# Larger pieces for the adding transfers of a decoder trunk, and a later start of their second group

## The chip, the cores and the metric

The kernel runs on one core of a Trainium2 chip. The metric is the time of one execution on the device in microseconds (us). Besides, one execution was recorded by the hardware profiler; all views quoted below come from that recording.

The engines go by these names: PE multiplies matrices (PEld is its loading of weights), DVE and ACT work elementwise, POOL is the general engine, which here does small column arithmetic and issues some DMA transfers, and SP issues the other transfers. Each engine takes its instructions strictly in the order of its own list; between engines there are only semaphores. "SPq", "ACTq" and "POOLq" mark issues of transfers. All transfers run on the same 16 DMA engines.

## The reference: what is computed

A trunk of two layers over 512 positions of width 1024, everything in float32:

```python
for i in range(DEPTH):                      # DEPTH = 2
    mixer, pre, post = (even_mixer, ...) if i % 2 == 0 else (odd_mixer, ...)
    x = x + rms_norm(mixer(rms_norm(x, pre)), post)
    h = conv_ffn(rms_norm(x, ffn_pre_g[i]), ffn_w_up[i], ffn_conv_w[i], ffn_conv_b[i], ffn_w_down[i])
    x = x + rms_norm(h, ffn_post_g[i])
```

The first mixer joins latent attention (8 heads) and differential attention (4 heads, where two softmaxes are subtracted and each head's output is normalised). The second joins dilated attention (three groups of 4 heads) and stick-breaking attention (4 heads). Each feed-forward block multiplies by `ffn_w_up` (1024 x 5632), applies a causal convolution of width 3, a gate, and `ffn_w_down` (2816 x 1024).

## The kernel before

**Products.** The 512 positions are four row tiles of 128, worked in the order 3, 2, 1, 0. Each float32 operand is split into a rounded high part and a remainder, and a product is three matmuls: high by high, high by low, low by high (`mm3`, L315 to L317). Weights come in units of up to 128 x 1024 floats. SP loads a unit into one of three raw buffers `wraw` (L59, or L57 for a unit of two halves), ACT rounds it into `wh` (L81), DVE subtracts to get `wl` (L82). Five pairs of `wh` and `wl` rotate, so that units are made ahead of use.

**The sums of weight blocks.** For some column tiles of `ffn_w_up` (14 pairs of tiles in layer 0, 12 in layer 1) the block product is done with seven products in place of eight. For that it needs four sums of blocks of these weights. They don't depend on x, and no engine computes them: DMA transfers that add into their destination build them, from one DRAM array (`in_ffn_up_q`) into others (`ws`), long before the feed-forward block reads them through L57. `sum_steps` (L145) lists the transfers. Pairs go in chunks of three, and for each chunk there are eight steps, four that copy and four that add:

```python
steps = [(0, 3, ALU.bypass), (2, 2, ALU.bypass), (0, 2, ALU.add), (2, 0, ALU.add), (1, None, ALU.bypass),
         (1, 0, ALU.add), (3, -1, ALU.bypass), (3, 1, ALU.add)]
```

The list runs step by step, and within a step over the chunks; a step waits for the earlier step on the same chunk. A transfer of a full chunk has 384 rows of 512 floats, which is 768 KB; the last chunk of layer 0 has two pairs, 512 KB. All of them are issued by POOL (L161), because adding transfers are issued there. `max_dma_last_dim` at the issue bounds the length of a piece in bytes. The descriptors that POOL writes for its transfers lie in a space of 1024 bytes, which the kernel sets when it is built (`dynamic_dma_scratch_size=1024`, L1918).

**Where they are issued.** Layer 0 (the first group): `make_sums(0, range(3))` puts the 24 transfers of three chunks into POOL's list in one run, after the normalisation of the latent columns in the first mixer (L1074). The other 16, of two chunks, are put one by one among the work units of differential attention. Layer 1 (the second group): `make_sums(1, range(CHUNKS[1]))`, 32 transfers of four chunks, in one call at L1493, between the first value tiles of the second mixer and its projections. A call begins with a "mark" (L168): a transfer of one float from some tile to the first `ws` chunk. It carries no data that matters; it holds the copies after it back until that tile is written. Before, the second group's mark reads a word of `xl`, the low part of the normalised and transposed x, in the columns of row tile 3, the first of the four to be written.

**What else POOL does.** `rstd` (L226) computes (mean square + eps)^-0.5 of a row tile on POOL: L230, L232 with a second half, L233. Differential attention does the same for each head and row tile (L1262, L1263); the result scales the output on DVE (L1270). At the change from the first feed-forward block to the second mixer, each row tile needs two: one for the block's output (then DVE adds it to x, L815) and one for the next input (then DVE scales it, L819, PE transposes it, L263, ACT and DVE split it into `xh` and `xl`, L223 and L224). These transposes stand among the matmuls of the first value tiles of the second mixer (`av`, one for each row tile; ACT takes each to `vst`, L1484, and sends it on by four transfers, L1486).

The order of POOL's list is written out by hand there (`manual_schedule`) or follows from the program's order and a planner's priorities. In the second group, the mark and the first seven transfers stood among the `rstd` instructions of row tiles 2, 1 and 0.

Of the kernel before, what the change touches and what calls it, by code (L numbers as in the profile page):

```python
# [9 lines left out]
F32 = mybir.dt.float32  # L10
# [7 lines left out]
P = 128  # L18
# [21 lines left out]
CHUNKS = [-(-n // CHUNK) for n in PAIRS]  # L40
# [55 lines left out]
def trunk(tc, A, out):  # L96
    nc = tc.nc
    PE, ACT, DVE, POOL = nc.tensor, nc.scalar, nc.vector, nc.gpsimd

    with ExitStack() as top:  # L100
# [28 lines left out]
        lead = cst.tile([P, 80], F32, tag="lead", name="lead")  # L129
# [15 lines left out]
        def sum_steps(layer, chunks, mark=None):  # L145

            wide = "(a q) c -> a (q c)"
            if layer not in sums_of:
                sums_of[layer] = [[dpool.tile([CHUNK * P, S], F32, tag=f"ws{layer}{j}{c}", name="ws")
                                   for c in range(CHUNKS[layer])] for j in range(4)]  # L150
            tiles = sums_of[layer]

            def move(c, j, src, op):
                n = min(CHUNK, PAIRS[layer] - c * CHUNK) * P
                if src is None:
                    src = tiles[0][c][:n]
                elif src < 0:
                    src = tiles[1][c][:n]
                else:
                    src = A[f"ffn_up_q{layer}"][src, c * CHUNK * P:c * CHUNK * P + n]  # L160
                nc.gpsimd.dma_start(tiles[j][c][:n].rearrange(wide, q=4), src.rearrange(wide, q=4), accum_op=op,  # L161
                                    max_dma_last_dim=2048)

            steps = [(0, 3, ALU.bypass), (2, 2, ALU.bypass), (0, 2, ALU.add), (2, 0, ALU.add), (1, None, ALU.bypass),
                     (1, 0, ALU.add), (3, -1, ALU.bypass), (3, 1, ALU.add)]
            moves = [lambda c=c, step=step: move(c, *step) for step in steps for c in chunks]
            if mark is not None:
                moves.insert(0, lambda: nc.gpsimd.dma_start(tiles[0][chunks[0]][0:1, 0:1], mark))  # L168
            return moves

        def make_sums(layer, chunks, mark):
            with tc.manual_schedule(engines={POOL.engine}):
                for move in sum_steps(layer, chunks, mark):
                    move()
# [1233 lines left out]
        def odd(xnT, pending, order):  # L1408
            xh, xl = xnT
            with ExitStack() as es:  # L1410
# [59 lines left out]
                for i in ORDER:  # L1470
# [12 lines left out]
                    st = chp.tile([P, 512], F32, tag="s", name="vst")  # L1483
# [6 lines left out]
                nc.scalar.dma_start(tab12[:], A["dil_tab12"])  # L1490
                DVE.tensor_copy(tri[:], trif[:])

                make_sums(1, range(CHUNKS[1]), xl[0:1, 0, 3 * P:3 * P + 1].bitcast(F32))  # L1493


                for u in range(2):
# [321 lines left out]
        xnT = even()  # L1818
        xnT = ffn(0, *xnT, False)
        xnT = odd(*xnT)  # L1820
        ffn(1, *xnT, True)

# [103 lines left out]
```

## Time and profile before

| | |
|---|---|
| median of 3 runs | 1184.62 us (1179.21 to 1190.16) |
| the profiled execution | 1182.12 us, span 1180.3 us |
| mean granted PE clock | 0.983 of full |
| PE busy | 1122.2 us, 95% of the span |
| DVE, ACT, POOL busy | 888.1, 629.8, 118.2 us |
| moved by DMA | 201.48 MB, mean 171 GB/s |
| issued by POOL | 72 transfers of sums and 2 marks |

The span is what the profile covers; the time of the same execution is 1.8 us longer. POOL's rows show when it issued a transfer and for how long. "issue" as the end of a wait means that the engine waited for nothing that the profile shows. Columns are explained where rows are quoted.

### The profile page before, as it was taken

What the parts mean: (1) busy time and instruction counts of PE and PEld (TensorE: products, weight loads), DVE (VectorE), ACT (ScalarE), POOL (GpSimd) and SP (SyncE); (2) the same over time, 40 slices, a digit from 0 to 9 for tenths busy, and PEclk for the clock granted to TensorE, in tenths of its full rate; (3) what the DMA queues carried; (4) which work ended last, traced back from release to release, by engine and by line L of the source; (5) the groups of instructions that cost most, each with busy time, mean ns of one, the idle gap of its engine ahead of it and who ended that gap; (6) DMA issues with size and microseconds to landing.
All of it is one profiled execution on the core that took longest, in us unless ns stands there. A gap on an engine that the chain in (4) does not pass through costs nothing.

```text
span 1180.3 us, 17608 instructions
## 1 busy us (share of the span) xinstructions
PE 1122.2 (95%) x6576; PEld 959.9 (81%) x6576; DVE 888.1 (75%) x1504; ACT 629.8 (53%) x1069; POOL 118.2 (10%) x213
## 2 busy tenths in 40 slices
PE   9999909889999999999997999999999999999997
PEld 8876706668899999888886887787989999888886
DVE  6686506528989999988984357566898999879887
ACT  5565506425656666455653355465466666535562
POOL 2211013232000000000023011111100000000001
PEclk9999959989999999999999999999999999999999
DMA  7777867764345656334658987787234655424462
GB/s 285 249 163 160 223 149 221 150 146 147 90 145 178 192 177 190 106 132 143 195 182 275 262 186 209 176 215 170 95 123 146 191 183 178 144 76 143 147 210 76
DMA packets 79541, 201.48 MB, mean 171 GB/s; under 512 B 9056, under 2 KB 10208, under 8 KB 79328
## 3 DMA queue, kind: packets, MB, share of 16 engines
q1 hardware_dynamic: 56352, 142.09, 36.9%
q0 software_dynamic: 21184, 54.53, 21.2%
q10 hardware_dynamic: 1920, 3.74, 1.0%
q8 instruction: 52, 0.85, 0.3%
q14 instruction: 33, 0.27, 0.1%
HBM read 192.95 MB, written 60.85 MB: 215 GB/s over the span
## 4 chain that ended last, share of the span: by engine, by line
PE 74%; issue 16%; POOL 4%; DMA 3%; DVE 1%; ACT 1%; SPq 0%; POOLq 0%; DVEq 0%; ACTq 0%
PE u L315 12%; PE u L317 12%; PE u L316 12%; PE acc L315 6%; PE acc L316 6%; PE acc L317 6%; PE apt L315 2%; PE apt L316 2%; PE apt L317 2%; POOL ws L161 2%; PE ao L317 1%; PE ao L315 1%; PE ao L316 1%; DMA ws<-ws 1%; PE p L317 1%
## 5 line engine op out<-in xcount | busy, mean ns | idle before, releaser
L81 ACT CAST wh<-wraw 128x1024 fp32r<-128x1024 f32 x237 | 245.1, 1047 | 155.7 <-PE u L316 50.0
L82 DVE TENSOR_TENSOR wl<-wraw,wh 128x1024 fp32r<-128x1024 f32 x237 | 287.0, 1219 | 51.4 <-ACT wh L81 50.8
L315 PE MATMUL u<-xh,wh 128*128 128x256 f32 (+1 forms) x664 | 212.0, 319 | 0.0
L316 PE MATMUL u<-xl,wh 128*128 128x256 f32 (+1 forms) x664 | 211.8, 319 | 0.0
L317 PE MATMUL u<-xh,wl 128*128 128x256 f32 (+1 forms) x664 | 211.7, 319 | 0.0
L317 PEld LDWEIGHTS u<-xh,wl 128*128 128x128 f32 x664 | 126.5, 190 | 9.0 <-DVE wl L82 0.3
L315 PEld LDWEIGHTS u<-xh,wh 128*128 128x128 f32 x664 | 126.5, 190 | 8.9 <-ACT wh L81 0.3
L316 PEld LDWEIGHTS u<-xl,wh 128*128 128x128 f32 x664 | 126.5, 190 | 8.7
L317 PE MATMUL acc<-wh,gl 128*128 128x512 f32 (+1 forms) x250 | 96.8, 387 | 0.0
L316 PE MATMUL acc<-wl,gh 128*128 128x512 f32 (+1 forms) x250 | 96.8, 387 | 0.0
L315 PE MATMUL acc<-wh,gh 128*128 128x512 f32 (+1 forms) x250 | 96.8, 388 | 0.0
L317 PE MATMUL u<-gh,wl 128*128 128x256 f32 x312 | 88.3, 283 | 0.0
L315 PE MATMUL u<-gh,wh 128*128 128x256 f32 x312 | 88.3, 283 | 0.0
L316 PE MATMUL u<-gl,wh 128*128 128x256 f32 x312 | 88.3, 283 | 0.0
L230 POOL TENSOR_TENSOR rv<-ms,epst 128x1 f32<-128x1 f32 x39 | 12.7, 326 | 697.4 <-ACT junk L755 320.4
L492 ACT ACTIVATE y<-u,cw 128x512 f32<-128x512 f32 x88 | 67.5, 775 | 14.6 <-PE u L317 14.6
L161 POOL DMA_DIRECT2D ws<-in_ffn_up_q x54 | 46.5, 861 | 282.0 <-issue 271.8
L496 DVE SCALAR_TENSOR_TENSOR y<-u,cw,y 128x511 f32<-128x511 f32 x88 | 65.0, 742 | 6.3 <-ACT y L492 6.3
L498 DVE SCALAR_TENSOR_TENSOR y<-u,cw,y 128x510 f32<-128x510 f32 x88 | 65.5, 746 | 2.3
L315 PEld LDWEIGHTS u<-gh,wh 128*128 128x128 f32 x312 | 59.9, 192 | 0.2
L316 PEld LDWEIGHTS u<-gl,wh 128*128 128x128 f32 x312 | 59.9, 192 | 0.1
L317 PEld LDWEIGHTS u<-gh,wl 128*128 128x128 f32 x312 | 59.9, 192 | 0.0
(362 smaller groups left out, 2456.9 us busy)
## 6 DMA issues: line engine op xcount, KB each, us to landing
ws<-in_ffn_up_q POOLq DMA_DIRECT2D x48, 768.0 KB, 7.3
wraw<-ws SPq DMA_DIRECT2D x104, 256.0 KB, 2.9
wraw<-in_ffn_w_down SPq DMA_DIRECT2D x44, 512.0 KB, 3.5
wraw<-in_ffn_up_q SPq DMA_DIRECT2D x78, 256.0 KB, 2.8
wraw<-in_ffn_w_up SPq DMA_DIRECT2D x36, 512.0 KB, 4.2
ws<-ws POOLq DMA_DIRECT2D x16, 768.0 KB, 6.0
wraw<-in_od_w_dqk SPq DMA_DIRECT2D x12, 512.0 KB, 5.9
wraw<-in_ffn_w_down SPq DMA_DIRECT2D x22, 256.0 KB, 2.9
```

The lines of the kernel that those rows point to most:

```text
L81: self.nc.scalar.copy(h[:, :w], raw[:, :w])
L82: self.nc.vector.tensor_tensor(l[:, :w], raw[:, :w], h[:, :w].bitcast(F32), ALU.subtract)
L161: nc.gpsimd.dma_start(tiles[j][c][:n].rearrange(wide, q=4), src.rearrange(wide, q=4), accum_op=op, max_dma_last_dim=2048)
L230: POOL.tensor_tensor(v[:, :n], ms, epst[:, :n], ALU.add)
L315: PE.matmul(o, lh, rh, start=first, stop=False, skip_group_check=more)
L316: PE.matmul(o, lh, rl, start=False, stop=False, skip_group_check=more)
L317: PE.matmul(o, ll, rh, start=False, stop=last, skip_group_check=more)
L492: ACT.activation(y[:, z], u[z], AF.Identity, bias=c[:, 3:4], scale=c[:, 2:3])
L496: DVE.scalar_tensor_tensor(y[:, z, 1:], u[z][:, :S - 1], c[:, 1:2], y[:, z, 1:], ALU.mult, ALU.add)
L498: DVE.scalar_tensor_tensor(y[:, z, 2:], u[z][:, :S - 2], c[:, 0:1], y[:, z, 2:], ALU.mult, ALU.add)
```

## The change

```diff
@@ sum_steps.move
                 nc.gpsimd.dma_start(tiles[j][c][:n].rearrange(wide, q=4), src.rearrange(wide, q=4), accum_op=op,
-                                    max_dma_last_dim=2048)
+                                    max_dma_last_dim=8192)
...
@@ odd, ahead of the second mixer's projections
                 DVE.tensor_copy(tri[:], trif[:])
 
-                make_sums(1, range(CHUNKS[1]), xl[0:1, 0, 3 * P:3 * P + 1].bitcast(F32))
+                ACT.copy(lead[0:1, 1:2], st[0:1, 0:1])
+                make_sums(1, range(CHUNKS[1]), lead[0:1, 1:2])
```

The first edit changes the bound on a piece from 2 KB to 8 KB for all transfers of `sum_steps`; four rows of 512 floats, which lie one behind another, then make one piece, and a full chunk is 96 rows of 2048 floats. The number of transfers, their bytes and their order among themselves stay.

The second edit changes what the second group waits for. `st` is the tile of the last `av` (row tile 0). ACT copies one float of it into a free column of the constant tile `lead`, after it has sent that tile on, and the mark reads that. In POOL's list the mark and all 32 transfers then stand behind the last `rstd` of the change of layers, in one run; before, the mark and seven transfers stood among those. ACT gains one instruction. The lists of PE, DVE and SP hold the same instructions in the same order.

## The prediction

> **What bounds the kernel now.** I read the page first: the busy times and the two rows of slices (each slice is 29.5 us).
>
> ```profile
> span 1180.3 us, 17608 instructions
> PE 1122.2 (95%) x6576; PEld 959.9 (81%) x6576; DVE 888.1 (75%) x1504; ACT 629.8 (53%) x1069; POOL 118.2 (10%) x213
> PE   9999909889999999999997999999999999999997
> PEclk9999959989999999999999999999999999999999
> ```
>
> PE is the bound nearly everywhere. It is idle for 1180.3 - 1122.2 = 58 us, and the slices say where: the sixth (147 to 177 us) has digit 0, the three after it 9, 8, 8, and the slice at 620 to 649 us has 7. The clock row dips at the same places. The view by windows puts numbers on them; after the window come its length, the busy time of PE, PEld, DVE, ACT, POOL, the granted clock, the DMA engines' busy share, and GB/s.
>
> ```profile
> 147.00:176.00 29.00, 1.66 (x8) 1.04 (x6) 0.73 (x4) 0.00 (x0) 5.58 (x9) 0.60 0.65 153
> 176.00:262.00 86.00, 73.35 (x351) 54.07 (x352) 40.64 (x117) 39.42 (x121) 26.98 (x49) 0.94 0.75 175
> 620.00:650.00 30.00, 23.22 (x105) 18.14 (x104) 14.01 (x19) 9.02 (x17) 9.04 (x17) 0.94 0.84 276
> ```
>
> PE's idle time is 27.3, 12.7 and 6.8 us, together 46.8 of the 58. Both places lie in the two groups of weight sums. Who keeps PE waiting is in the view of waits (engine, what it was about to do, what ended the wait: total us, times, longest).
>
> ```profile
> DVE otok L1270 <- POOL rr L1263: 56.7, 8, 30.4
> PE tpp L906 <- DVE s L1245: 33.3, 4, 27.8
> PE tpp L906 <- DVE odl L224: 5.2, 2, 3.5
> PE tpo L1277 <- DVE otok L1270: 2.1, 1, 2.1
> DVE t L819 <- POOL rr L233: 10.6, 3, 6.0
> PE av L317 <- DVE xl L224: 3.4, 1, 3.4
> ```
>
> At both places DVE waits for an `rr` of POOL, and PE for DVE. The timeline of the first place:
>
> ```profile
> 140.97 0.19 ACT L1260 ACTIVATION_READ_ACCUMULATOR jk<-otok 128x1 f32 x1
> 148.26 0.40 PE L317 MATMUL aqk<-xh,wl 128*128 128x512 f32 x1
> 158.26 0.98 POOL L161 DMA_DIRECT2D ws<-in_ffn_up_q  x1 [4.89 <-issue]
> 166.04 0.97 POOL L161 DMA_DIRECT2D ws<-in_ffn_up_q  x1 [6.80 <-issue]
> 173.20 0.95 POOL L161 DMA_DIRECT2D ws<-in_ffn_up_q  x1 [6.18 <-issue]
> 174.34 0.18 POOL L1262 TENSOR_TENSOR st<-st,epsp 128x1 f32<-128x1 f32 x1
> 175.20 0.35 DVE L1270 SCALAR_TENSOR_TENSOR otok<-otok,rr,subg 128x128 f32<-128x128 f32 x1 [30.36 <-POOL rr L1263]
> ```
>
> ACT has the sum of squares ready at 141.16. POOL takes it up at 174.34, because 24 issues of sums stand ahead of it. DVE, which takes its list in order, stops at the result, and PE runs dry at 148.7. **So the kernel's main loss is POOL's queue of issues, not DMA speed as such.**
>
> **Part 1, larger pieces: why POOL's issues are slow.**
>
> ```profile
> q0 software_dynamic: 21184, 54.53, 21.2%
> ws<-in_ffn_up_q POOLq DMA_DIRECT2D x48, 768.0 KB, 7.3
> 86.39 1.05 POOL L161 DMA_DIRECT2D ws<-in_ffn_up_q  x1 [6.08 <-issue]
> 93.81 0.95 POOL L161 DMA_DIRECT2D ws<-in_ffn_up_q  x1 [6.36 <-issue]
> 219.26 0.93 POOL L161 DMA_DIRECT2D ws<-in_ffn_up_q  x1 [5.05 <-issue]
> 221.01 0.69 POOL L161 DMA_DIRECT2D ws<-ws  x1
> 42.00:61.00 19.00, 19.00 (x85) 15.75 (x84) 7.89 (x11) 7.44 (x12) 2.60 (x5) 1.00 0.86 304
> 81.00:86.00 5.00, 5.00 (x24) 3.22 (x23) 4.45 (x16) 2.98 (x9) 0.00 (x0) 1.00 0.95 157
> ```
>
> The first row is a queue with its packets, MB and share of the engines; the second an issue with its count, size and median us to landing. The packet count fits one reading exactly. The 26 pairs give 104 copying moves of 256 KB and 104 adding ones. Copies in 4 KB and adds in 2 KB are 104 x 64 + 104 x 128 = 19968 packets, and 76 queued transfers with 16 completion writes make 21184. A full adding transfer is thus 384 pieces, 24 for each DMA engine, 25 with the completion.
>
> Two such adds never overlap: issues are 7.4 us apart (86.39, 93.81), as long as the median landing of 7.3. Yet POOL doesn't wait for an add as such: at 221.01 a copy of 384 rows is issued 1.75 us after an add of 256 rows (16 pieces an engine, 17 with the completion), far below any landing. So it is room for descriptors that is short: 25 + 25 don't fit, 17 + 13 do. With 8 KB an add takes 6 + 1 an engine, and even 30 hold four. I take it that up to four adds then queue up, POOL runs ahead, and the DMA engines work without gaps.
>
> The price of an add on the engines themselves is unknown for 8 KB. At 81 to 86 us adds run alone: 157 GB/s at 0.95 busy, so 768 KB (0.786 MB) take 5.0 us. The low end is a copy's rate, 304 GB/s in the window of copies, 2.6 us; the high end is the whole spacing of 7.4 us, no gain. I take 5.0: the same bytes are read and written, and 2 KB pieces leave the engines at 0.95.
>
> ```profile
> 61.00:173.00 112.00, 86.81 (x418) 59.10 (x416) 57.91 (x201) 48.26 (x133) 14.43 (x17) 0.91 0.75 176
> 657.00:817.00 160.00, 159.01 (x981) 128.87 (x981) 98.37 (x239) 84.06 (x149) 18.52 (x23) 1.00 0.82 202
> ```
>
> First group: from the first add to the last issue the DMA engines do 0.75 x 112 = 84 us of work, sums and weights together. With three adds in the queue rather than one, POOL issues the last one 2 x 5.0 = 10 us of work earlier: 74. At 0.95 occupancy that is 61 + 78 = 139 us, in place of 173. The `rr` is wanted from 141.2, and DVE has nothing else from 175.20 - 30.36 = 144.8. So the stall goes, by a margin of 2 to 6 us. If each of the ten adds up to there takes 1 us more, POOL is free near 149, and about 4 us stay. In the later stretch, 176 to 262, one issue stands behind each unit; small adds fit beside one another there, and POOL's waits go too.
>
> What is recovered is PE's idle time, 27.3 + 12.7 = 40.0, and the slow clock after it: a mean of 0.94 over 86 us is 10 us at half speed, of which PE is busy 73.35/86, 8.8, costing 4.4; the first window adds at most 0.8. Next in line are waits inside attention, PE for `odl` and `otok`, 5.2 + 2.1 = 7.3 us; I leave them standing, though POOL's delays feed them. **40.0 + 5.2 - 7.3 = 38 us.**
>
> **Part 2, the later start.**
>
> ```profile
> 629.48 1.41 DVE L819 SCALAR_TENSOR_TENSOR t<-X,rr,gain 128x512 f32<-128x512 f32 x2 [3.96 <-POOL rr L233]
> 644.12 1.42 DVE L819 SCALAR_TENSOR_TENSOR t<-X,rr,gain 128x512 f32<-128x512 f32 x2 [5.97 <-POOL rr L233]
> 622.72 1.29 POOL L161 DMA_DIRECT2D ws<-in_ffn_up_q  x2 [1.50 <-DMA ws<-xl]
> 655.06 3.48 ACTq L1486 DMA_DIRECT2D cv<-vst  x4
> 658.58 2.00 ACT L81 CAST wh<-wraw 128x1024 fp32r<-128x1024 f32 x2 [3.88 <-issue]
> 816.80 0.95 POOL L161 DMA_DIRECT2D ws<-in_ffn_up_q  x1 [10.77 <-issue]
> 817.50 0.20 ACT L282 ACTIVATION_READ_ACCUMULATOR junk<-ao 128x1 f32 x1
> 854.76 0.37 SPq L57 DMA_DIRECT2D wraw<-ws  x1
> ```
>
> It removes from the change of layers the issues that stand among the `rr`s. DVE's 3.96 and 5.97 us end, and 6.8 us of PE's idle time with them. The clock of 0.94 over 30 us is 3.6 us at half speed, 2.8 of it busy, costing 1.4. **6.8 + 1.4 = 8 us.** The chain of norms itself is then a few tenths for each POOL step; nothing else is late there.
>
> It adds one ACT copy of one float. The nearest row is the 128x1 readout, 0.20 us; from nothing to 0.6 (a whole 128x512 evict) I take 0.2. Two roundings of weights stand behind it (658.58), which follow a pause of 3.88 us on ACT, and in 657 to 817 PE is busy for 159.01 of 160 us: hidden. If that cover failed, it would cost its own 0.2.
>
> It moves the mark behind 655.06 + 3.48 + 0.2 = 658.7, and the first copies some 3.5 us later, 662.3 in place of 622.72. POOL's list holds behind the mark only the sums and then the `rstd` of the second mixer's output, whose input is ready at 817.70. So the 32 transfers must have been issued by then. DMA work: 0.82 x 160 = 131 us from 657 on, plus the eight copies that used to run earlier (8 x 0.786 MB at 304 GB/s = 21 us), minus three more adds in the queue (15): 137. At 0.97 occupancy POOL is free at 662.3 + 141 = 803, 14 us early. The thirteen adds up to there may each take 1.1 us more before POOL is late. `ws` is first read at 854.76, and all has landed by about 825. SP's list is not moved; its loads for the value tiles lose the copies beside them, those for the projections gain adds.
>
> **Sum.** 38 + 8 = 46. The profiled execution took 1182.12 us, the span 1180.3 with 1.8 around it: 1182.1 - 46 = 1136. It lies 2.5 us below the median of the three runs, so I forecast **1139 us**.
>
> **Rivals.** (a) *Late weights.* A piece of 8 KB holds a DMA engine for 5.0/6 = 0.83 us in place of 0.21.
>
> ```profile
> q1 hardware_dynamic: 56352, 142.09, 36.9%
> 660.92 57.49 SPq L59 DMA_DIRECT2D wraw<-in_od_w_dqk  x12
> ```
>
> The weights' queue took 0.369 x 1180.3 x 16 / 56352 = 0.124 us for a packet of 2.5 KB, so 4 KB take 0.2. If the engines alternate between queues piece by piece, weights get 16 x 4 KB in 1.03 us, 64 GB/s, while adds are queued. Twelve units of 512 KB are called for in 57.5 us: 109 GB/s. Over the eight adds beside them, some 45 us, the weights would fall 45 x 0.045 = 2.0 MB short, 32 us at that rate. Against it: eight units, 4.2 MB, are buffered (five split, three raw), so it decides only where fewer than four of them are full. The Trainium skill's page "DMA: Bandwidth & Descriptors", section Queues, rings and completion order, states that each engine goes round its queues packet by packet, and a whole packet is drained before it switches; that is this rival's rule, and no row of before shows it for pieces of 8 KB. Its price lies between nothing and 32 us; I take half, 1155.
>
> (b) *Adds still go one at a time*, because POOL waits for something in an add other than room. For it: no two full adds overlap anywhere. Against it: 221.01. The first group gains nothing; the second keeps its 194 us from first to last issue but starts 39.6 later, so POOL is free at 856 and the output norm, wanted at 817.7, is 39 us late; 8 are won at the start. 1184.6 + 31 = 1216. Today's margin is 817.70 - 816.80 = 0.9 us, so any delay beyond that counts; it turns the kernel slower once the group's 194 us shrink by less than 39.6 - 0.9 - 8 = 31 us and the first group gains nothing.
>
> (c) *The pieces relieve the first group in part* (an add takes 6 to 7 us): 10 to 25 us of the gain are lost at both places, 1150 to 1165.
>
> (d) *Pieces aren't larger on the engines*, because the issue cuts them again. Then (b)'s delay meets nothing gained, the same 1216; I count it with (b).
>
> **How the numbers follow.** Forecast as worked out, 1128 to 1150: 0.66. (a) and (c), up to 1165: 0.20. Slower, (b) and (d): 0.10. Partial gains that cancel the later start, near 1180: 0.04. The lowest time takes all the idle and clock loss of the three windows, 46.8 + 6.6 = 53.4: 1182.1 - 53.4 = 1129, and I go to 1128; the upper end is 1160, inside (a) and (c). About 1% is what a measurement of this kernel can tell from no change (the three runs span 0.9%). Faster by over 1%: 0.86, within: 0.04, slower: 0.10.
>
> **What would show it.** Right: no 30 us wait of `otok` for `rr`; POOL's issues of full adds under 6 us apart or in bunches, the last of the first run before 145 us; the slow clock near 150 us gone; no PE wait at `av`; POOL's last issue of the second group before the output norm asks. Wrong: issues still 7 us apart, a wait of DVE for `rr` after the second mixer, or ACT waiting for `wraw` in the second mixer's projections.

## The result, and the profile after

The changed kernel takes **1135.04 us** (median of 4 runs, 1134.66 to 1136.26), the kernel before 1183.5 us (4 runs, 1179.21 to 1190.16). The ratio is 0.9588 with a 95% interval of 0.9541 to 0.9634: faster by 4.1%. The forecast was 1139 us.

The profiled execution after took 1134.86 us. From its page, the span, the busy times, and PE's and the clock's rows of slices (a slice is now 28.3 us):

```profile
span 1133.1 us, 17611 instructions
PE 1115.9 (98%) x6576; PEld 957.3 (84%) x6576; DVE 889.1 (78%) x1504; ACT 631.5 (56%) x1070; POOL 108.1 (10%) x213
PE   9979999999999999999999999999999999999997
PEclk9989999999999999999999999999999999999999
```

The slice with digit 0 and the one with 7 are gone, and the clock no longer dips there. Instead the third slice has 7, with a clock of 8 in the same slice; before, both were 9. PE's idle time fell from 58.1 to 1133.1 - 1115.9 = 17.2 us, which is 40.9, and its busy time by 1122.2 - 1115.9 = 6.3 us with the same 6576 matmuls, because fewer of them ran at a low clock (mean granted 0.983 before, 0.995 after). Together that is 47.2 us, the whole difference of the two spans.

The view by windows for the same places (columns as in the prediction), and for the new one:

```profile
64.00:90.00 26.00, 19.17 (x83) 12.69 (x82) 13.58 (x57) 9.25 (x31) 3.19 (x6) 0.87 1.02 280
147.00:176.00 29.00, 29.00 (x156) 21.10 (x155) 19.15 (x56) 19.47 (x55) 8.94 (x18) 1.00 0.74 209
176.00:262.00 86.00, 85.58 (x490) 69.75 (x489) 55.91 (x112) 43.58 (x114) 25.26 (x51) 1.00 0.59 164
640.00:780.00 140.00, 139.31 (x855) 111.11 (x852) 93.82 (x237) 80.13 (x149) 17.30 (x29) 1.00 0.77 213
```

At 147 to 262 us PE is full and the clock too. Who keeps PE waiting now, in the view of waits; this row is the longest, and the next one is 1.1 us:

```profile
PE sps L1111 <- DVE st L895: 6.8, 1, 6.8
```

POOL's timeline shows why `otok` no longer waits. The rows are issues of sums up to 112.61, then the first norm of differential attention, the second group with its mark, and the first norm of the second mixer's output; after the start come its duration, the instruction, and the idle time before it:

```profile
58.54 0.79 POOL L161 DMA_DIRECT2D ws<-in_ffn_up_q  x1 [5.18 <-issue]
64.34 0.79 POOL L161 DMA_DIRECT2D ws<-in_ffn_up_q  x1 [5.01 <-issue]
...
112.61 0.79 POOL L161 DMA_DIRECT2D ws<-in_ffn_up_q  x1 [1.86 <-DMA ws<-ws]
149.14 0.19 POOL L1262 TENSOR_TENSOR st<-st,epsp 128x1 f32<-128x1 f32 x1 [35.63 <-ACT jk L1260]
609.78 0.63 POOL L168 DMA_DIRECT2D ws<-lead  x1 [14.86 <-ACT lead L1493]
613.96 4.07 POOL L161 DMA_DIRECT2D ws<-in_ffn_up_q  x8 [3.55 <-DMA ws<-lead]
...
718.73 0.79 POOL L161 DMA_DIRECT2D ws<-in_ffn_up_q  x1 [2.00 <-DMA ws<-ws]
768.36 0.19 POOL L230 TENSOR_TENSOR rv<-ms,epst 128x1 f32<-128x1 f32 x1 [48.85 <-ACT junk L282]
```

Before, POOL reached this norm 33 us late. Now POOL waits 35.63 us for ACT, not the other way round. The second run ends at 718.73, and POOL then waits 48.85 us for ACT, at the change to the second mixer's output norm. Full adds are issued some 6 us apart here in place of 7.4 (58.54 to 64.34).

The new stall is one tile. ACT issues the load of the latent attention's mask, `mmask`, at 61.47 us (62.1 before). It landed in 2.9 us before, and in 11.0 us after. DVE's and PE's timelines after:

```profile
72.66 0.29 DVE L895 CUSTOM_DVE_ANT_0 s<-sps,mmask 128x128 f32<-128x128 f32 x1 [7.58 <-DMA mmask<-in_mla_mask]
73.02 2.07 PE L1111 MATMUL sps<-mk,mq 128*128 128x256 f32 x4 [6.83 <-DVE st L895]
```

The same window of before shows what changed around it:

```profile
64.00:90.00 26.00, 25.94 (x126) 17.21 (x124) 21.34 (x87) 15.13 (x51) 2.98 (x3) 1.00 0.78 161
```

The DMA engines were 0.78 busy at 161 GB/s while one add was under way at a time; now they are full, at 280 GB/s, and a small load stands among the adds.

### The profile page after: what moved, and what is told of

It reads as the page before. It is cut to its first block, busy times and chain, and to the rows that moved or that the text cites. A ratio compares the mean times of both kernels' runs of the same rounds, so it can differ in the third digit from the quotient of the medians.

```text
span 1133.1 us, 17611 instructions
## 1 busy us (share of the span) xinstructions
PE 1115.9 (98%) x6576; PEld 957.3 (84%) x6576; DVE 889.1 (78%) x1504; ACT 631.5 (56%) x1070; POOL 108.1 (10%) x213
## 3 DMA queue, kind: packets, MB, share of 16 engines
q0 software_dynamic: 7872, 54.53, 18.7%
## 4 chain that ended last, share of the span: by engine, by line
PE 90%; issue 3%; DMA 3%; POOL 1%; DVE 1%; ACT 1%; SPq 0%; POOLq 0%; DVEq 0%; ACTq 0%
PE u L317 12%; PE u L315 12%; PE u L316 12%; PE acc L315 6%; PE acc L317 6%; PE acc L316 6%; PE apt L315 3%; PE apt L316 3%; PE apt L317 2%; PE sps L1111 2%; PE ao L317 1%; PE ao L315 1%; PE ao L316 1%; PE av L317 1%; PE av L316 1%
## 5 line engine op out<-in xcount | busy, mean ns | idle before, releaser
L315 PEld LDWEIGHTS acc<-wh,gh 128*128 128x128 f32 x250 | 46.9, 188 | 10.1 <-issue 0.5
## 6 DMA issues: line engine op xcount, KB each, us to landing
ws<-in_ffn_up_q POOLq DMA_DIRECT2D x48, 768.0 KB, 15.3
```

Source lines behind the costliest of these rows:

```text
L315: PE.matmul(o, lh, rh, start=first, stop=False, skip_group_check=more)
```

## The experiments

**Second edit alone**: pieces stay at 2 KB, the second group starts late.

```diff
+                ACT.copy(lead[0:1, 1:2], st[0:1, 0:1])
+                make_sums(1, range(CHUNKS[1]), lead[0:1, 1:2])
```

> The second edit alone: pieces of 2 KB, the second group starts at the last value tile. The prediction's working: POOL still issues one add at a time, the second group starts some 40 us later and keeps its 194 us, so POOL is about 39 us late for the second mixer's output norm, and 8 us are won at the change of layers: about 1216 us, PE idle near 820 us, and the 30 us stall near 150 us stays. Rival (the later start alone does the second group's part, because the transfers meet less traffic later): the group shrinks by more than 30 us, 1175 to 1185.

Measured: 1213.16 us in a single run, the kernel before 1181.84 in a single run beside it, 31.3 us slower. Waits of PE:

```profile
PE tpp L906 <- DVE s L1245: 40.1, 3, 37.5
PE tp L263 <- DVE t L1783: 26.9, 1, 26.9
```

The first stall is still there, and a second one stands at the second mixer's output. This is rival (b)'s slow case: the late start is only to be had once POOL issues faster. That the loss meets the price worked out for it (31 us) so closely is partly luck. At the second mixer's output DVE's longest wait for `rr` was 29.2 us, where the working had 39; and the first stall is about 10 us longer than in the profile of before (27.8), though the edit changes nothing there.

**Pieces of 4 KB** with both edits.

```diff
-                                    max_dma_last_dim=2048)
+                                    max_dma_last_dim=4096)
```

> Both edits with pieces of 4 KB. If an add takes one descriptor a piece (12 + 1 an engine), four fit as with 8 KB and the time is that of the change, 1133 to 1142 us. If it takes three a piece, as the issues of the 8 KB run suggest (three adds and a copy fit together, four adds don't; eight copies do: 3 x 19 + 7 = 64), a 4 KB add takes 37 and two (74) don't fit in 64: adds go one at a time again, spaced 6 us or more, the first group relieves POOL near 150 us only, the second is late: 1150 to 1210 us.

Measured: 1132.14 us in a single run, 1 us below the range of the first expectation. POOL's queue (packets, MB, share of the engines), then the longest wait of PE:

```profile
q0 software_dynamic: 14528, 54.53, 19.9%
```

```profile
PE sps L1111 <- DVE st L895: 4.8, 1, 4.8
```

The packets are 208 x 64 + 1216 = 14528, all moves in 4 KB. The first run of issues ended at 121.19 us. So 4 KB is enough to free POOL, and a count of descriptors by which it would not have been is wrong.

**More room for descriptors, pieces unchanged.** The kernel before with a space of 2048 bytes. To make place for it, the scratch tile `ra` has one buffer in place of two, `lead` is cut to two columns, and the mask is loaded into a tile of differential attention (`dk[3]`) that is free until then; nothing of the computation changes.

```diff
-    nc = bacc.Bacc("TRN2", target_bir_lowering=False, num_devices=1, dynamic_dma_scratch_size=1024)
+    nc = bacc.Bacc("TRN2", target_bir_lowering=False, num_devices=1, dynamic_dma_scratch_size=2048)
```

> The kernel before (2 KB, early start) with descriptor space of 2048 bytes in place of 1024; to make room for it, the rotary helper has one buffer in place of two, the constant tile lead is 2 columns wide, and the mask of latent attention lies in an attention tile that is free then, loaded with the constants. If an add takes one descriptor a piece (25), five adds fit in 128, POOL runs ahead and most of the first group's gain is there without larger pieces: 1140 to 1152 us. If it takes three a piece (73), two still don't fit and only copies behind an add are issued earlier: 1172 to 1186 us. If POOL waits for adds for another reason than room: 1180 to 1186 us.

Measured: 1141.34 us in a single run, 40.5 below the kernel before (1181.84). POOL's queue, PE's longest wait, and of POOL's first run the first copies and the last issue:

```profile
q0 software_dynamic: 21184, 54.53, 20.9%
```

```profile
PE av L315 <- ACT xh L223: 4.8, 1, 4.8
```

```profile
39.77 2.97 POOL L161 DMA_DIRECT2D ws<-in_ffn_up_q  x5 [2.68 <-DMA ws<-rr]
...
124.01 0.94 POOL L161 DMA_DIRECT2D ws<-in_ffn_up_q  x1 [7.43 <-PE av L317]
```

The packets are those of before, 21184, and the stall of 30 us is gone all the same: five copies go out at once where two did before, and the run ends at 124.01 in place of 173.20. The mask's earlier load can't be what took this stall away: before, the mask landed in 2.9 us and no engine waited for it. So room was what held POOL back. Longer pieces are one way to make room, and a larger space another.

**First edit alone**: pieces of 8 KB, early start.

```diff
-                                    max_dma_last_dim=2048)
+                                    max_dma_last_dim=8192)
```

> The first edit alone: pieces of 8 KB, the second group starts at row tile 3 of xl as before. The prediction gave the later start 8 us of its own (6.8 us of PE idle time and 1.4 of clock at the change of layers): 1143 us, with DVE waiting for rr at L819. Rival: the 8 us come from the pieces too, because all eight copies now fit in the queue and POOL passes them in half a microsecond each: 1134 to 1138 us, no PE wait at av.

Measured: 1164.63 us (1163.81 to 1167.28), ratio 0.9812 with an interval of 0.9763 to 0.9862. Both expectations missed it, by 20 us or more. The first group's waits are those of the changed kernel; the loss is at the change of layers. Four views follow: PE's waits (two rows); issues with their count, size and median us to landing; windows; ACT's timeline.

```profile
PE apt L317 <- DVE wl L82: 10.0, 1, 10.0
PE sps L1111 <- DVE st L895: 7.2, 1, 7.2
```

```profile
cv<-vst ACTq DMA_DIRECT2D x16, 64.0 KB, 12.3
trif<-in_sb_tri ACTq DMA_DIRECT2D x1, 128.0 KB, 19.6
```

```profile
600.00:620.00 20.00, 15.07 (x57) 11.85 (x56) 3.74 (x4) 5.57 (x8) 2.36 (x3) 0.83 1.02 308
620.00:640.00 20.00, 9.97 (x36) 7.74 (x35) 3.70 (x4) 2.48 (x3) 3.97 (x6) 0.70 1.04 241
640.00:660.00 20.00, 16.05 (x84) 14.16 (x83) 5.46 (x6) 4.68 (x5) 2.95 (x4) 0.87 1.03 344
```

```profile
620.59 7.02 ACTq L1486 DMA_DIRECT2D cv<-vst  x4
627.65 1.99 ACT L81 CAST wh<-wraw 128x1024 fp32r<-128x1024 f32 x2 [10.39 <-DMA cv<-vst]
645.85 1.05 ACT L81 CAST wh<-wraw 128x1024 fp32r<-128x1024 f32 x1 [15.71 <-DMA wraw<-in_od_w_v]
```

In these 60 us PE is idle for 60 - 41.1 = 18.9 us, and its busy time loses 15.07 x 0.17 + 9.97 x 0.30 + 16.05 x 0.13 = 7.6 us to the clock: 26.5 of the 29.3 us between this kernel and the changed one, whose PE has no such waits at the change of layers. Small loads come late here at two places. ACT, which rounds the weights, stops at the value tiles' transfers (median landing 12.3 us, 6.0 before and 4.2 after). And DVE stops at `trif`, a constant of 128 KB that lands 19.6 us after its issue (6.2 before, 3.7 after). Three units of weights stand behind that in DVE's list, and PE's longest stall ends with the first of them. Two rows of DVE and one of PE:

```profile
634.01 0.29 DVE L1491 CAST tri<-trif 128x256 fp32r<-128x256 f32 x1 [16.93 <-DMA trif<-in_sb_tri]
634.22 3.49 DVE L82 TENSOR_TENSOR wl<-wraw,wh 128x1024 fp32r<-128x1024 f32 x3
635.50 0.80 PE L317 MATMUL apt<-xh,wl 128*128 128x512 f32 x1 [10.03 <-DVE wl L82]
```

The unit for which ACT then waits 15.71 us is late for the same reason: SP waited up to 15.0 us for DVE's `wl` before it could load the next unit. No run loads `trif` earlier, so how much of the loss goes with it alone isn't shown. With both edits the sums are not yet queued when these transfers run. The late start is therefore worth 29 us with pieces of 8 KB, not 8.

**First edit for the adds only**, early start; copies keep the bound of 2 KB and their 4 KB packets. It tells the eight copies at the front of the group from the adds behind them.

```diff
-                                    max_dma_last_dim=2048)
+                                    max_dma_last_dim=2048 if op == ALU.bypass else 8192)
```

> The first edit alone, for adds only: adds in 8 KB, copies in 2 KB rows as before, early start of the second group. The first edit alone lost 29 us against both edits, with the transfers of the value tiles landing late (12.3 us in place of 4.2). If the eight copies queued at once do that, they go two at a time here again and most of the loss goes: 1138 to 1148 us, but POOL waits among the norms for room as before. If the long adds after them do it: 1158 to 1168 us.

Measured: 1167.0 us (1166.45 to 1168.98), ratio 0.984 (0.9808 to 0.9872), the same stall in PE's waits and in the landings:

```profile
PE apt L317 <- DVE wl L82: 11.4, 1, 11.4
```

```profile
cv<-vst ACTq DMA_DIRECT2D x16, 64.0 KB, 10.0
```

DVE waited 20.6 us for `trif` here, and PE 8.5 us among the norms besides. The length of the copies is not the cause; the long adds suffice. The kernel with more room, above, also starts the group early, and its adds of 2 KB run ahead too; there the value tiles' transfers landed in 7.4 us and `trif` in 8.6, and PE's longest wait was 4.8 us. So the large loss goes with the 8 KB adds. Whether it is the length of their pieces or the number of them under way, and by which step an add delays a value tile's transfer, isn't shown by these runs.

**The changed kernel again, with its mask loaded early.** SP loads the mask into `dk[3]` behind the table `qtab`, ahead of the sums, in place of ACT's load among them.

```diff
                         nc.sync.dma_start(qtab[:], A["rope_q"])
+                        mmask = dk[3]
+                        nc.sync.dma_start(mmask, A["mla_mask"])
...
-                    mmask = sc.tile([P, S], F32, tag="mmask", name="mmask")
-                    nc.scalar.dma_start(mmask[:], A["mla_mask"])
```

> The changed kernel itself, to be compared with the other kernels of this call on the same chip: 1134 to 1137 us.

> The changed kernel with the mask of latent attention loaded with the constants, ahead of the first group, into an attention tile that is free until then. Theory: the new 6.8 us stall of PE near 66 us is the mask's load queued behind sums (11.0 us to landing where it took 2.9); without it the idle time and the half clock behind it (6.8 us, costing 3) go: 1125 us. Rival: another load that is queued behind the sums takes its place at once: 1131 to 1135 us.

Measured on one chip: the changed kernel 1135.33 us (1134.47 to 1135.67), ratio 0.9561 (0.9505 to 0.9617); with the early mask **1127.95 us** (1127.63 to 1128.67), ratio 0.9501 (0.9454 to 0.9547). The ranges of the two don't touch; the mask cost 7.4 us. This is the fastest kernel of the study. PE's longest wait, and PE's row of slices:

```profile
PE warm L926 <- DVE dqk L872: 1.1, 1, 1.1
```

```profile
PE   9999999999999999999999999999999999999997
```

**The sums behind the mask instead**: the first group's mark reads the mask, so that the sums start once it has landed.

```diff
-                        make_sums(0, range(3), rk[0:1, 0:1])
...
                     nc.scalar.dma_start(mmask[:], A["mla_mask"])
+                    make_sums(0, range(3), mmask[0:1, 0:1])
```

> The changed kernel with the first group's mark reading the mask, so that the group starts only when the mask has landed, some 25 us later. Theory: the mask lands in 3 us, POOL's run of 24 issues ends near 138 us in place of 113, still ahead of the first normalisation near 142: 1125 us. Rival: the sums now meet the loads for differential attention, or POOL is late: a few us of waits of otok for rr, 1128 to 1140 us.

Measured: 1141.7 us (1136.64 to 1142.34), ratio 0.9606 (0.9555 to 0.9657). That is above both expectations. The stall moved on to the next loads, those of differential attention; POOL was not late for its norms. PE's longest wait, and the landings:

```profile
PE sps L1227 <- DVE st L1231: 6.3, 1, 6.3
```

```profile
alibi<-in_alibi ACTq DMA_DIRECT2D x1, 1024.0 KB, 19.0
subg<-in_ev_subln_g ACTq DMA_DIRECT2D x1, 64.0 KB, 10.3
```

They landed in 7.1 and 2.8 us in the changed kernel. A later start of the first group moves the collision; an earlier load of the mask removes it.

**Early mask with pieces of 4 KB**, and **early mask and late start with pieces of 2 KB and a space of 2048 bytes**.

```diff
-                                    max_dma_last_dim=8192)
+                                    max_dma_last_dim=4096)
```

> The changed kernel with pieces of 4 KB in place of 8 KB and the mask of latent attention loaded ahead of the first group. Theory: pieces of 4 KB already let POOL run far enough ahead, and hold up other loads less (weights for the dilated projections landed in 7.8 us beside them, 11.0 beside 8 KB, 5.9 beside 2 KB); as PE is now idle almost nowhere, the time is that of 8 KB with the early mask, 1126 to 1129 us. Rival: POOL, which issues the last of the first run at 121 in place of 113 us, is late: 1130 to 1135 us.

> Pieces of 2 KB, the later start, descriptor space of 2048 bytes and the early mask (rotary helper with one buffer, lead with 2 columns). If room alone is what mattered, long pieces aren't needed: the first group gains as in the run with room alone, the late start protects the value tiles, 1128 to 1136 us. If long pieces carry part of the gain by their faster rate (18.7% of the engines' span in place of 21.2%), the second group ends late for the output norm: 1140 to 1165 us.

Measured: 1131.18 us (1127.78 to 1132.36), ratio 0.953 (0.9496 to 0.9564), and 1134.95 us (1128.84 to 1136.35), ratio 0.9552 (0.9506 to 0.9599). The first lies above its theory's range and in the rival's, but POOL was not late there: it issued the last transfer of the first run at 123.06, and the norm came at 145.85. The second lies in the range for room alone. The intervals of these two and of the 8 KB kernel with the early mask overlap. So room, however it is made, a late start and the early mask together come within a few us of the fastest kernel with pieces of any of the three lengths; whether 8 KB is better than 4 KB by 3 us isn't settled. In the kernel with 2 KB and more room, PE's longest wait and the end of POOL's second run:

```profile
PE tpp L906 <- DVE s L1245: 5.5, 1, 5.5
```

```profile
737.46 0.96 POOL L161 DMA_DIRECT2D ws<-in_ffn_up_q  x1 [3.90 <-issue]
768.74 0.19 POOL L230 TENSOR_TENSOR rv<-ms,epst 128x1 f32<-128x1 f32 x1 [30.32 <-ACT junk L282]
```

POOL's second run ends 30 us ahead of the output norm here, 49 us ahead with pieces of 8 KB (718.73 above).

## Why the prediction was right, step by step

- **"The kernel's main loss is POOL's queue of issues."** Shown. With 2 KB pieces and more room (and the mask moved out of the way) the wait of 30 us was gone and the time 40.5 us lower, in a single run.
- **Room for descriptors, not waiting for an add as such.** Shown by the same run, against rival (b). The count behind it holds only in part. "Up to four adds queue up" was too many: transfers of sums took 15.3 us to land (median of the row below, 32 of whose 48 are adds) and were issued some 6 us apart, so between two and three were under way. What one add takes of the space stays open; the 4 KB kernel ran ahead although the reading tried there said that it could not.

Issues of the changed kernel with their median us to landing, and POOL's queue:

```profile
ws<-in_ffn_up_q POOLq DMA_DIRECT2D x48, 768.0 KB, 15.3
wraw<-in_od_w_dqk SPq DMA_DIRECT2D x12, 512.0 KB, 11.0
...
q0 software_dynamic: 7872, 54.53, 18.7%
```

- **The pieces.** The packets are 208 x 32 + 1216 = 7872, so the pieces did get larger, against rival (d). The copies became 8 KB too, where the prediction only spoke of adds. The remainder of 1216 is the same with pieces of 2, 4 and 8 KB, but the 76 transfers it was put down to aren't shown: the profile counts 74 issues by POOL. The longer copies changed nothing that was forecast; the run with copies left at 4 KB stalled as the one with 8 KB did.
- **The add at 5.0 us on the engines.** Near: the queue's engine time for all sums fell from 0.212 x 1180.3 = 250 to 0.187 x 1133.1 = 212 us, 15% less. Part of that isn't the pieces: with more room and the late start, 2 KB pieces took 0.211 x 1133.6 = 239 us, against which 8 KB saves 11%.
- **First group, last issue at 139 us.** It was 112.6, 26 us earlier. The step that missed is "84 us of work": it put all transfers of those 112 us ahead of the last issue, weights too, and the sums at their old price. In the changed kernel the engines are 1.00 busy from 61 to 112.6, that is 51.6 us, and 0.58 busy from 112.6 to 147, another 20 us. By the shares of the queues in these windows, loads other than sums took 17 us of the 84 before; after, 5 us of them ran ahead of the last issue and 10 behind it. The sums took 0.600 x 112 = 67 us before and 0.900 x 51.6 + 0.284 x 34.4 = 56 after, of which 10 were still under way behind the last issue, as the prediction had it. So about 12 us of the miss are other loads that didn't stand in POOL's way, and about 11 are cheaper sums. Windows of the changed kernel:

```profile
61.00:112.60 51.60, 44.71 (x207) 29.28 (x207) 33.64 (x133) 25.68 (x80) 8.76 (x13) 0.93 1.00 260
112.60:147.00 34.40, 34.37 (x164) 24.08 (x160) 20.38 (x59) 17.30 (x39) 0.90 (x2) 1.00 0.58 157
```

- **38 us at the first group.** 40.0 idle, 5.2 clock: both came. The 7.3 us of waits for `odl` and `otok` that were left standing went too, since POOL was free; in their place stood the wait for the mask, 6.8 us of idle time and 19.17 x 0.13 = 2.5 us of clock, that no step had named. **Two misses of about the same size cancelled, so it is partly luck that the time came within 4 us of the forecast.** Without the second the time would have been that with the early mask, 1127.95, 11 us under the forecast and just below the range's low end of 1128.
- **8 us for the later start.** Right for the difference to the kernel before, where waits for `rr` went. Against the same pieces started early, it is 29 us. The late start undoes a cost that the first edit makes.
- **Second group, POOL free at 803.** It was at 719.5, 49 us ahead of the norm in place of 14. Everything runs some 47 us earlier by then, and the group itself took 105 us (614 to 719) in place of 141, for the reasons given for the first: ahead of the last issue other loads took 23 us of the engines' time where the working had 40, and the sums 84 where it had 98.
- **Rival (a), late weights.** The loads of `od_w_dqk` beside the adds landed in 5.9 us before; with the late start and adds that ran ahead, in 7.9 us with 2 KB pieces (and more room), 7.8 with 4 KB (8.5 with the early mask), and 11.0 with 8 KB (10.3 with the early mask). The Trainium skill, page "DMA: Bandwidth & Descriptors", section Queues, rings and completion order, has an engine go round its queues a packet at a time. The traces agree with that in direction only: 8 KB pieces go with later landings, but between 2 and 4 KB none is clearly later. A part of the delay thus comes with a fuller queue, and a part goes with 8 KB pieces. In the second mixer's projections five made and three raw units covered it, as the prediction said against it: PE was busy for 139.31 of 140 us. Loads that land late beside the adds did decide elsewhere: at a mask without any buffer ahead of it, and, in the kernel with the early start, at the value tiles and at `trif`.

## What to carry to other kernels

An engine that issues transfers and also does small arithmetic is a place where a full descriptor space turns into a stall of everyone else; look for issues that stand as far apart as one transfer takes to land, and try both longer pieces and more room. Once such a queue runs full, small loads that share the DMA engines with it can land several times later (here the mask in 11.0 us in place of 2.9, `trif` in 19.6 in place of 3.7): list those that are issued just in time, and load them ahead of the burst. Moving the burst is less sure: in the first group it only found the next loads, in the second it was worth 29 us. And when two edits are made together, price each with the other present: here the late start loses 31 us alone, in a single run of which about ten stand where it changes nothing, and is worth 29 us beside the long pieces.

## What was not expected of the hardware

- A load of 256 KB took 11.0 us beside adds in 8 KB pieces, 9.0 beside 4 KB and 2.9 beside adds that went one at a time (the mask's landings).
- Four issues of 64 KB transfers on ACT (620.59 above) spread over 7.02 us beside the early adds of 8 KB, where the same four took 3.48 us before and 2.41 after. Whether the issue itself was slow or ACT waited between them, the profile doesn't show.
